# Sixteen tokens moved from the dense to the gathered path, and half of the experts' weight loads issued from ScalarE's queue

## The chip, the cores and the metric

The kernel runs on one core of a Trainium2 chip. The metric is device time in microseconds (us); the median of three runs of the kernel before is 2014.75 us (2012.73 to 2016.01). The engines are TensorE (PE, with its weight loads shown apart as PEld), VectorE (DVE), ScalarE (ACT), GpSimd (POOL) and SyncE (SP).

## The reference

One inference step of a one-layer transformer on 288 tokens (256 prompt tokens, 32 sampled ones) of width 2048 in float32: differential attention with a relative bias, cross-attention into 256 memory tokens, output projection, a first norm, and then a product-key expert layer:

```
q = (x1 @ w_q) -> 8 heads x 2 halves; s = q . sub_keys          # 128 keys in each half
16 best of each half -> 16 best of their 256 sums: expert = 128 * i1 + i2; gates = softmax(best)
act = x1 . u[expert]; h = gelu(act) * gate; y = sum h * v[expert]     # 128 experts of 16384 per token
out = layer_norm(ALPHA * x1 + y)
```

The tables u and v have 16384 rows of 2048 numbers each.

## The kernel before

Weights stream from DRAM in units of 128 x 1024 floats, 512 KB each, in the fixed order of the list `plan`. A unit goes through `raw` (four buffers, loaded by `load_next`), then ScalarE rounds it into `hi` (L165) and VectorE takes the rest into `lo` (L181), three buffers each; TensorE multiplies both, so that float32 is kept with the fast type. `take` gives TensorE the next unit; before that `stream` has emitted the `hi` of the unit two ahead and the loads of the units up to four ahead. A load waits until the `lo` of the unit four before it has been made, because they share a buffer. In the kernel before SP issues all these loads.

The expert layer treats the tokens in two ways.

- The dense tokens, ND = 224 of them, are multiplied with all experts. The key blocks i = 0 to 127 are two units each: 16 times a product of 448 columns (L1039, both parts of the tokens against `hi`) and one of 224 (L1041, against `lo`). `finish_act` adds the small products with a product by the identity (`small`, L992; L994) and applies gelu. From block 64 on (G0) `gate_jobs` spreads the gates over all experts, two tokens per unit: VectorE makes the one-hot rows of the second key, ScalarE makes those of the first by two activations a token (L974, L975), TensorE multiplies them, and `gate_in` puts the gates of four tokens into the activations (`bigA`, `bigB`): multiplied by VectorE where the activation is there, copied by VectorE where it is not. Then come 256 units of values, V: 8 pairs of products a unit (L1200, L1202) onto eight accumulators, in two halves of the columns.
- The other 64 tokens are gathered: for each of 64 slots, POOL fetches the two half rows of 128 experts (64 tokens by two groups of heads fill the 128 partitions) by an indirect DMA (L948), 512 KB a step and 128 steps for u and again for v, into three buffers; VectorE multiplies each with the token's row (`use_u`, L963) or adds it to `vacc` (`use_v`, L1111). The steps are spread evenly over the units by `upto`: GFIRST = 40 of u before block 64, the others until block 126, and those of v from about unit 9 to unit VEND = 230.

Beside the stream, `slow` holds work that VectorE does in small pieces, paced once per tick by an estimated cost: the top-16 search (`topk`), the choices, and at the end `finish_gathered`, which adds the halves of the gathered tokens, norms and stores them. It is begun when the last step of v has been emitted, and what is left of it is emitted at once in the last group of V (three units), ahead of the evacuation of the last eight accumulators (L1120). The norm rows of the dense tokens are loaded by it too, into `vacc`, and the last stage (`centred`, `finished`, `store`) needs them.

In `order`'s rows below, `hi_5<-raw_4` is the rounding of a unit, `DMA raw_4<-in_v` its load, `ohA` a first-key one-hot, `small` and `tmp` the steps of `finish_act`, `vr` a gathered half row, `x1g` the gathered tokens' rows (later `vacc`), `x1b` those of the added ones.

Of the kernel before, what the change touches and what calls it, by code (L numbers as in the profile page):

```python
# [21 lines left out]
ND = 224  # L22
# [13 lines left out]
SPLIT = 96  # L36
# [7 lines left out]
GFIRST = 40  # L44
# [5 lines left out]
def tile_stream_step(ctx: ExitStack, tc, xT_d, xn_d, memT_d, ckT_d, cv_d, cmkT_d, cmv_d,  # L50
# [54 lines left out]
    # ------------------------------------------------ the stream of everything large  # L105
# [36 lines left out]
    plan += [weight(wq_d[t, half]) for t in Q_TILES[2:] for half in range(2)]  # L142
    plan += [weight(ut_d[i, half]) for i in range(NKEY) for half in range(2)]
# [5 lines left out]
    def stream(n, ahead=AHEAD):  # L149
        """splits up to the weights that are ahead units after unit n, and loads beyond them"""  # L150
# [78 lines left out]
    def mm_tile(ps, part, k, d, mh, ml, n):  # L229
        """out^T [128 columns, n tokens] += one contraction tile of weights' (mh + ml)"""  # L230
# [5 lines left out]
    def mm_unit(ps, half, mh, ml, n, ticks=(3, 7), tiles=8):  # L236
        """the next unit's contraction tiles"""
# [54 lines left out]
    def bias_job():  # L292
        """the relative bias of all heads, laid out by diagonals through DRAM"""
# [35 lines left out]
    # ------------------------------------------------ mixers  # L329
# [45 lines left out]
    def diff_attend(h, qT, kT, vT, ck, cv):  # L375
# [51 lines left out]
        def weights(t):  # L427
            # w * s0 = e0 - lam * s0 / s1 * e1
# [155 lines left out]
    # ------------------------------------------------ output projection, first norm  # L584
# [27 lines left out]
    def residual(c, ps):  # L612
        """the tokens' rows again, added to the residual"""
# [3 lines left out]
                       ps[:, ND:NTOK].unsqueeze(1).to_broadcast([P, 2, 64]))  # L617
# [44 lines left out]
    # ------------------------------------------------ expert choice  # L662
    ROWS = (P, 96, P)

    def topk(units):
# [3 lines left out]
        st = []  # L669
        for q, (t, h, u) in enumerate(units):  # L670
            R = ROWS[t]

            def new(tag, shape, dt=F32, share=None, q=q, R=R, t=t, h=h):
                return tw.tile([P] + shape, dt, tag=f"{share or tag}{q}", name=f"{tag}{t}_{h}")[:R]
            st.append(dict(R=R, s=s_all[:R, u], sv=new("sv", [2, K]), si=new("si", [2, K], U32), sf=new("sf", [2, K]),
                           s2=new("s2", [2, NKEY]), ca=new("ca", [K, K]), new=new, pos=new("pos", [K], U32),
                           ab=new("ab", [2, K], U32), abf=new("abf", [2, K]), bv=best[:R, t, h],
                           en=(e1n[:R, t, h], e2n[:R, t, h])))
        n = len(units)
        both = [(x, c) for c in range(2) for x in st]  # L680
        for x, c in both:
            V.max(out=x["sv"][:, c, 0:8], in_=x["s"][:, c])
        for x, c in both:
            V.max_index(out=x["si"][:, c, 0:8], in_max=x["sv"][:, c, 0:8], in_values=x["s"][:, c])
            if c == 0 and x is st[-1]:
# [9 lines left out]
        for x, c in both:
            V.max_index(out=x["si"][:, c, 8:16], in_max=x["sv"][:, c, 8:16], in_values=x["s2"][:, c])
        for x in st:
            R = x["R"]
            V.tensor_tensor(out=x["ca"], in0=x["sv"][:, 0].unsqueeze(2).to_broadcast([R, K, K]),
                            in1=x["sv"][:, 1].unsqueeze(1).to_broadcast([R, K, K]), op=OP.add)  # L700
        yield 0.75 * n
        for x in st:
            V.tensor_copy(x["sf"], x["si"])
            x["cb"] = x["new"]("cb", [K, K], share="s2")
            x["cf"], x["c2"] = (x[k].rearrange("p a b -> p (a b)") for k in ("ca", "cb"))
        for x in st:
            V.max(out=x["bv"][:, 0:8], in_=x["cf"])
        yield 0.45 * n
        for x in st:
            V.match_replace(out=x["c2"], in_to_replace=x["bv"][:, 0:8], in_values=x["cf"], imm_value=-3.0e38)  # L710
        for x in st:
            V.max_index(out=x["pos"][:, 0:8], in_max=x["bv"][:, 0:8], in_values=x["cf"])
# [680 lines left out]
```

## Time and profile before

| | |
|---|---|
| median of three runs | 2014.75 us |
| span of the profiled execution, first to last instruction | 2008.1 us; that leaves 6.65 us to the median |
| busy: PE, PEld, DVE, ACT, POOL | 99%, 93%, 78%, 58%, 24% of the span |
| key blocks | first product 624.6 us; first gate product, in block 64, 960.4 us |
| values V | 1336 to 1990 us, the last stage to 2008.1 us |
| DMA, whole span | 521.21 MB, 260 GB/s |

A line of the page or of an answer names the line of the kernel, the engine, the operation and the tiles. "Idle before" is the time for which an engine waited ahead of an instruction, and the name behind the arrow is what ended that wait. A table by windows shows, for each stretch, the busy time of every engine with its count of instructions, the granted clock of TensorE as a share of full speed, the mean busy share of the 16 DMA engines and the rate at which they moved data.

### The profile page before, as it was taken

To read this page: it belongs to the slowest core of one execution; us is meant where nothing else is said; L and a number is where in the kernel's file an instruction comes from. 1 tells how busy PE (TensorE), PEld (TensorE's weight loads), DVE (VectorE), ACT (ScalarE), POOL (GpSimd) and SP (SyncE) were. 2 spreads that over 40 slices of the span, in tenths; PEclk is the share of its full clock that TensorE was granted. 3 is DMA by queue.
4 is the path that set the end of the run, shared out by engine and by line. 5 is a ranking of instruction groups with operands and counts; after the bars stand their busy time and mean duration, and the time that the engine had idled before them with its cause. 6 is when DMAs were issued, how large, how long until landed. Compare 5 with 4: busy or idle time off the path is not lost.

```text
span 2008.1 us, 34989 instructions
## 1 busy us (share of the span) xinstructions
PE 1983.6 (99%) x13178; PEld 1872.5 (93%) x13178; DVE 1567.3 (78%) x2683; ACT 1160.7 (58%) x1919; POOL 480.9 (24%) x348
## 2 busy tenths in 40 slices
PE   9999999999999999999999999999999999999996
PEld 7999999999999999999999999999999999999996
DVE  5455555556788889998899999978888888888886
ACT  5345545544534555555999999854455555444553
POOL 0110000010000112222333333324443343334412
PEclk9999999999999999999999999999999999999998
DMA  8854555484445788888888888889999998999985
GB/s 294 258 165 141 153 155 153 129 287 137 154 148 162 241 291 280 277 282 283 294 298 296 293 298 302 300 288 318 335 322 343 327 333 314 323 328 321 327 264 167
DMA packets 147625, 521.21 MB, mean 260 GB/s; under 512 B 16848, under 2 KB 21088, under 8 KB 147328
## 3 DMA queue, kind: packets, MB, share of 16 engines
q1 hardware_dynamic: 103504, 360.49, 54.8%
q0 software_dynamic: 43952, 158.48, 22.0%
q8 instruction: 104, 1.70, 0.3%
q14 instruction: 65, 0.53, 0.1%
HBM read 508.33 MB, written 10.06 MB: 258 GB/s over the span
## 4 chain that ended last, share of the span: by engine, by line
PE 96%; DMA 1%; DVE 1%; ACT 1%; POOL 0%; issue 0%; SPq 0%; POOLq 0%; ACTq 0%; DVEq 0%
PE pa L1039 22%; PE pa L1200 11%; PE pb L1200 11%; PE pa L1041 11%; PE pa L232 8%; PE pa L233 7%; PE pa L234 7%; PE pb L1202 5%; PE pa L1202 5%; PE pb L1019 3%; DMA raw<-in_wmk 1%; PE pa L994 1%; PE pb L397 0%; DVE lo L181 0%; PE pa L893 0%; PE pa L319 0%
## 5 line engine op out<-in xcount | busy, mean ns | idle before, releaser
L181 DVE TENSOR_TENSOR lo<-raw,hi 128x1024 fp32r<-128x1024 f32 (+1 forms) x679 | 820.8, 1211 | 367.1 <-ACT hi L165 356.7
L165 ACT CAST hi<-raw 128x1024 fp32r<-128x1024 f32 (+1 forms) x679 | 705.5, 1040 | 497.2 <-PE pa L1200 253.8
L1039 PE MATMUL pa<-ux,hi 128*128 128x448 f32 x2048 | 669.8, 379 | 0.0
L1041 PE MATMUL pa<-ux,lo 128*128 128x224 f32 x2048 | 543.6, 265 | 0.0
L1039 PEld LDWEIGHTS pa<-ux,hi 128*128 128x128 f32 x2048 | 385.4, 188 | 29.4 <-issue 0.2
L1041 PEld LDWEIGHTS pa<-ux,lo 128*128 128x128 f32 x2048 | 391.7, 191 | 0.0
L948 POOL DMA_INDIRECT ur<-in_u,gidx x128 | 197.9, 1546 | 700.2 <-DVE ur L963 329.8
L1200 PE MATMUL pa<-hs,hi 128*128 128x448 f32 x1020 | 338.3, 376 | 0.0
L1200 PE MATMUL pb<-hs,hi 128*128 128x448 f32 x1020 | 338.0, 376 | 0.0
L948 POOL DMA_INDIRECT vr<-in_v,gidx x128 | 221.4, 1730 | 354.7 <-DVE x1g L1111 321.2
L1202 PE MATMUL pb<-hs,lo 128*128 128x224 f32 x1020 | 271.1, 266 | 0.3 <-DVE lo L181 0.3
L1202 PE MATMUL pa<-hs,lo 128*128 128x224 f32 x1020 | 271.0, 266 | 0.0
L1200 PEld LDWEIGHTS pb<-hs,hi 128*128 128x128 f32 x1020 | 191.4, 188 | 17.5
L1200 PEld LDWEIGHTS pa<-hs,hi 128*128 128x128 f32 x1020 | 191.4, 188 | 17.4
L1202 PEld LDWEIGHTS pb<-hs,lo 128*128 128x128 f32 x1020 | 195.1, 191 | 0.5 <-DVE lo L181 0.5
L232 PE MATMUL pa<-xh,hi 128*128 128x288 f32 x640 | 195.2, 305 | 0.0
L1202 PEld LDWEIGHTS pa<-hs,lo 128*128 128x128 f32 x1020 | 195.1, 191 | 0.0
L233 PE MATMUL pa<-xl,hi 128*128 128x288 f32 x640 | 188.9, 295 | 0.0
L234 PE MATMUL pa<-xh,lo 128*128 128x288 f32 x640 | 188.2, 294 | 0.0
L1111 DVE SCALAR_TENSOR_TENSOR x1g<-vr,ggate,x1g 128x1024 f32<-128x1024 f32 x128 | 163.7, 1279 | 0.0
L963 DVE SCALAR_TENSOR_TENSOR ur<-ur,x1g 128x1024 f32<-128x1024 f32 x128 | 155.7, 1216 | 0.0
L232 PEld LDWEIGHTS pa<-xh,hi 128*128 128x128 f32 x640 | 120.0, 188 | 4.9 <-issue 3.7
(346 smaller groups left out, 2706.7 us busy)
## 6 DMA issues: line engine op xcount, KB each, us to landing
raw<-in_ut SPq DMA_DIRECT2D x256, 512.0 KB, 4.4
raw<-in_v SPq DMA_DIRECT2D x255, 512.0 KB, 6.5
raw<-in_win SPq DMA_DIRECT2D x80, 512.0 KB, 3.7
raw<-in_wq SPq DMA_DIRECT2D x32, 512.0 KB, 3.6
raw<-in_wo SPq DMA_DIRECT2D x29, 512.0 KB, 3.7
raw<-in_wmv SPq DMA_DIRECT2D x8, 512.0 KB, 5.3
raw<-in_wmk SPq DMA_DIRECT2D x6, 512.0 KB, 5.8
xn<-in_xn POOLq DMA_DIRECT2D x8, 384.0 KB, 9.7
```

The source lines that it names most:

```text
L165: nc.scalar.copy(hi[:, cs], raw[:, cs])
L181: nc.vector.tensor_sub(lo, raw, hi.bitcast(F32))
L232: nc.tensor.matmul(ps[:, :n], wh, mh[:, d, :n], start=(d == 0), stop=False)
L233: nc.tensor.matmul(ps[:, :n], wh, ml[:, d, :n], start=False, stop=False)
L234: nc.tensor.matmul(ps[:, :n], wl, mh[:, d, :n], start=False, stop=(d == DT - 1))
L948: nc.gpsimd.indirect_dma_start(out=t, out_offset=None, in_=self.table, in_offset=bass.IndirectOffsetOnAxis(ap=gidx[:, a, s:s + 1], axis=0))
L963: nc.vector.scalar_tensor_tensor(rows, rows, 1.0, x1g[:, a * 1024:(a + 1) * 1024], op0=OP.mult, op1=OP.mult, accum_out=gact[:, a, s:s + 1])
L1039: nc.tensor.matmul(ps[:, :2 * ND], wh, ux[:, d].rearrange("p a t -> p (a t)"), start=(d == 0), stop=False, skip_group_check=True)
L1041: nc.tensor.matmul(ps[:, :ND], wl, ux[:, d, 0], start=False, stop=False, skip_group_check=True)
L1111: nc.vector.scalar_tensor_tensor(va, rows, ggate[:, s:s + 1], va, op0=OP.mult, op1=OP.add)
L1200: nc.tensor.matmul(accs[dt][:, :2 * ND], wh, hb.rearrange("p a t -> p (a t)"), start=(i == 0), stop=False, skip_group_check=True)
L1202: nc.tensor.matmul(accs[dt][:, :ND], wl, hb[:, 0], start=False, stop=False, skip_group_check=True)
```

## The change

ND becomes 208 and 80 tokens are gathered: the 64 of before, and the 16 tokens 208 to 223, each of which has its eight heads in eight groups of partitions and 16 further slots (`x1b`). There are 160 steps for u and for v instead of 128. The dense products have 416 and 208 columns instead of 448 and 224, and there are 104 gate jobs for two tokens instead of 112. The pieces of `topk` work on two heads in one instruction where they can; the second key's one-hots are made for four tokens at once; the copies of `gate_in` go from VectorE to ScalarE. `finish_gathered` has four foldings instead of one and a move of 16 rows. Every odd unit from the first key block on is loaded from ScalarE's queue.

```diff
-ND = 224
+ND = 208
+NA = 224
+SLOTS = 80
+STEPS = 2 * SLOTS
-SPLIT = 96
+SPLIT = 88
-GFIRST = 40
+GFIRST = 48
...
+    UFIRST = len(plan)
     plan += [weight(ut_d[i, half]) for i in range(NKEY) for half in range(2)]
...
+            queue = nc.scalar if k >= UFIRST and k % 2 else nc.sync
             for cs in pieces(k):
-                nc.sync.dma_start(raw[:, cs], src[:, cs])
+                queue.dma_start(raw[:, cs], src[:, cs])
...
     def gate_in(t0, ps, done):
...
             if a < n:
-                nc.vector.tensor_copy(bt[:, a:n, t0:t0 + 4], pg[:, i0 + a:i0 + n])
+                nc.scalar.copy(bt[:, a:n, t0:t0 + 4], pg[:, i0 + a:i0 + n])
...
+    def second_hots(t0):
+        Bt = big[2].tile([P, 4, NKEY], F32, tag="ohB", name=f"ohB{t0}")
+        nc.vector.tensor_tensor(out=Bt, in0=iota.unsqueeze(1).to_broadcast([P, 4, NKEY]),
+                                in1=e2T[:, t0:t0 + 4].unsqueeze(2).to_broadcast([P, 4, NKEY]), op=OP.is_equal)
+        return Bt
...
-                    ug.upto(GFIRST + (128 - GFIRST) * (n + 1 - 2 * G0) // (2 * (NKEY - G0) - 4))
+                    ug.upto(GFIRST + (STEPS - GFIRST) * (n + 1 - 2 * G0) // (2 * (NKEY - G0) - 4))
...
     def use_v(s, a, rows):
-        va = vacc[:, a * 1024:(a + 1) * 1024]
+        va = (vacc if s < 64 else x1b)[:, a * 1024:(a + 1) * 1024]
         nc.vector.scalar_tensor_tensor(va, rows, ggate[:, s:s + 1], va, op0=OP.mult, op1=OP.add)
...
     def finish_gathered():
-        up = [gat.tile([P, 1024], F32, tag="rows", name=f"up{c}") for c in range(2)]
-        for c in range(2):
-            nc.gpsimd.dma_start(up[c][:64], vacc[64:128, c * 1024:(c + 1) * 1024])
+        for x, w in ((vacc, 64), (x1b, 64), (x1b, 32), (x1b, 16)):
+            up = [gat.tile([P, 1024], F32, tag="rows", name=f"up{num()}") for c in range(2)]
+            for c in range(2):
+                nc.gpsimd.dma_start(up[c][:w], x[w:2 * w, c * 1024:(c + 1) * 1024])
+            yield 4.0
+            for c in range(2):
+                cs = slice(c * 1024, (c + 1) * 1024)
+                nc.vector.tensor_add(x[0:w, cs], x[0:w, cs], up[c][:w])
+                yield 1.15
+        nc.gpsimd.dma_start(vacc[64:SLOTS], x1b[0:16])
         yield 4.0
-        v = vacc[0:64]
...
+        v = vacc[0:SLOTS]
...
-                vg.upto(128 * (n + 1 - v_from) // (VEND - v_from))
+                vg.upto(STEPS * (n + 1 - v_from) // (VEND - v_from))
```

On ScalarE in the values, the kernel before has this order (one `hs` in four units):

```order
L165 CAST hi_16790<-raw_16743 128x1024
L165 CAST hi_16815<-raw_16768 128x1024
L165 CAST hi_16840<-raw_16793 128x1024
L165 CAST hi_16862<-raw_16818 128x1024
L75 CAST hs_16884<-bigA 128x4x224
```

and the changed kernel this one:

```order
L169 CAST hi_21056<-raw_21015 128x1024
L196 DMA raw_21059<-in_v 128x1024
L78 CAST hs_21079<-bigB 128x4x208
L169 CAST hi_21082<-raw_21037 128x1024
L169 CAST hi_21105<-raw_21059 128x1024
L196 DMA raw_21108<-in_v 128x1024
L169 CAST hi_21131<-raw_21085 128x1024
L169 CAST hi_21153<-raw_21108 128x1024
```

The load of each odd unit now stands behind the rounding of the odd unit ahead of it: raw_21108 is issued behind the instruction that reads raw_21059.

On ScalarE in the key blocks from 64 on, one block (two units) before:

```order
L992 CAST small_12880<-pa_12802 128x224
L165 CAST hi_12883<-raw_12806 128x1024
L1000 ACTIVATE tmp_12906<-pa_12802 128x112
L1002 ACTIVATE bigA<-pa_12802 128x112
L974 ACTIVATE ohA_12910<-iota,e1T 128x128
L975 ACTIVATE ohA_12910<-ohA_12910,gT,ngT 128x128
L974 ACTIVATE ohA_12910<-iota,e1T 128x128
L975 ACTIVATE ohA_12910<-ohA_12910,gT,ngT 128x128
L165 CAST hi_12918<-raw_12844 128x1024
```

and the second half of such a block in the changed kernel:

```order
L169 CAST hi_13076<-raw_13001 128x1024
L196 DMA raw_13079<-in_ut 128x1024
L981 ACTIVATE ohA_13099<-iota,e1T 128x128
L982 ACTIVATE ohA_13099<-ohA_13099,gT,ngT 128x128
L981 ACTIVATE ohA_13099<-iota,e1T 128x128
L982 ACTIVATE ohA_13099<-ohA_13099,gT,ngT 128x128
L994 COPY bigB<-pb_13026 128x31x4
L999 CAST small_13113<-pa_13037 128x208
```

A load and a copy of the gates (two of them below block 88) are new among ScalarE's instructions there; the copy waits for VectorE's multiplication out of the same bank.

On VectorE at the end of the values, the kernel before goes from the last `lo` to the accumulators:

```order
L181 TENSOR_TENSOR lo_21651<-raw_21604,hi_21650 128x1024
L181 TENSOR_TENSOR lo_21682<-raw_21629,hi_21681 128x1024
L181 TENSOR_TENSOR lo_21702<-raw_21653,hi_21701 128x256 x4
L1120 SCALAR_TENSOR_TENSOR yT<-yT,pb_18636 128x224
L1120 SCALAR_TENSOR_TENSOR yT<-yT,pb_18639 128x224
```

and the changed kernel, in two pieces with the norm's six smallest steps between them:

```order
L185 TENSOR_TENSOR lo_21512<-raw_21466,hi_21511 128x1024
L185 TENSOR_TENSOR lo_21532<-raw_21488,hi_21531 128x256 x4
L1161 TENSOR_TENSOR x1b<-x1b,up_21412 16x1024
L1169 BN_STATS nst_21545<-x1g 80x6 x4
L1143 BN_AGGR nmr_21546<-nst_21545 80x2
```

```order
L1145 SCALAR_TENSOR_TENSOR nmr_21546<-nmr_21546 80x1
L1179 TENSOR_TENSOR x1g<-x1g,gb_21543 80x1024
L1181 TENSOR_TENSOR x1g<-x1g,gb_21544 80x1024
L1179 TENSOR_TENSOR x1g<-x1g,gb_21568 80x1024
L1181 TENSOR_TENSOR x1g<-x1g,gb_21569 80x1024
L1135 SCALAR_TENSOR_TENSOR yT<-yT,pb_18445 128x208
```

The last folding and the whole norm of the gathered tokens stand ahead of the first accumulator's evacuation.

## Rows read from the trace of the kernel before

**Rows 1.** Busy time by stretch: the columns are us, engines, clock, DMA share, GB/s.

```profile
640.00:950.00 310.00, 310.00 (x1986) 294.64 (x1985) 275.88 (x650) 170.62 (x253) 58.37 (x41) 1.00 0.82 273
960.00:1290.00 330.00, 330.00 (x2235) 315.67 (x2234) 302.65 (x587) 310.25 (x708) 121.42 (x77) 1.00 0.85 297
1360.00:1640.00 280.00, 280.00 (x1770) 264.83 (x1770) 235.82 (x202) 139.66 (x139) 114.43 (x71) 1.00 0.94 331
1680.00:1900.00 220.00, 220.00 (x1391) 207.96 (x1390) 185.39 (x158) 110.14 (x109) 88.80 (x50) 1.00 0.93 326
```

**Rows 2.** Timeline of PE in three stretches: start, duration, instruction.

```profile
43.73 0.40 PE L320 MATMUL pa<-hi,meml 128*128 128x512 f32 x1
59.13 0.40 PE L320 MATMUL pa<-hi,meml 128*128 128x512 f32 x1
...
641.44 0.37 PE L1039 MATMUL pa<-ux,hi 128*128 128x448 f32 x1
645.82 0.37 PE L1039 MATMUL pa<-ux,hi 128*128 128x448 f32 x1
```

**Rows 3.** Timeline of ACT, key block 87 to 88.

```profile
1100.43 0.33 ACT L992 CAST small<-pa 128x224 fp32r<-128x224 f32 x1
...
1101.94 0.25 ACT L1000 ACTIVATE tmp<-pa 128x92 f32<-128x92 f32 x1 [0.23 <-PE pa L994]
...
1106.49 0.32 ACT L992 CAST small<-pa 128x224 fp32r<-128x224 f32 x1
```

**Rows 4.** Groups by line and shape, 1360 to 1640 us: count, busy, mean ns, idle before.

```profile
L181 DVE TENSOR_TENSOR lo<-raw,hi 128x1024 fp32r<-128x1024 f32 x111 | 135.9, 1225 | 44.2 <-ACT hi L165 40.8
L165 ACT CAST hi<-raw 128x1024 fp32r<-128x1024 f32 x111 | 116.8, 1052 | 140.8 <-PE pa L1200 109.7 <-DMA raw<-in_v 23.5 <-DVE lo L181 4.0
...
L1111 DVE SCALAR_TENSOR_TENSOR x1g<-vr,ggate,x1g 128x1024 f32<-128x1024 f32 x63 | 80.6, 1280 | 0.0
L76 DVE TENSOR_TENSOR hs<-bigA,hs 128x896 fp32r<-128x896 f32 x21 | 22.8, 1086 | 0.0
```

**Rows 5.** Busy time by stretch, two stretches of 20 us.

```profile
640.00:660.00 20.00, 20.00 (x130) 19.04 (x129) 19.30 (x59) 10.81 (x16) 0.00 (x0) 1.00 0.69 202
1420.00:1440.00 20.00, 20.00 (x129) 18.93 (x128) 16.19 (x14) 10.10 (x10) 8.42 (x6) 1.00 0.97 350
```

**Rows 6.** DMA issues, 1360 to 1640 us: count, KB each, median us to landing.

```profile
raw<-in_v SPq DMA_DIRECT2D x110, 512.0 KB, 6.7
```

**Rows 7.** DMA issues, 520 to 620 us.

```profile
raw<-in_wq SPq DMA_DIRECT2D x23, 512.0 KB, 3.6
```

**Rows 8.** Line 191, SP's queue, 1500 to 1520 us: duration ns min/median/max of one issue.

```profile
L191 SPq DMA_DIRECT2D raw<-in_v x8: 327/328/328, 1501.0 to 1519.6; - x8
```

**Rows 9.** Timeline of DVE at the end.

```profile
1939.46 0.26 DVE L1128 BATCH_NORM_AGGREGATE nmr<-nst 64x2 f32<-64x24 f32 x1
...
1942.21 0.15 DVE L1130 SCALAR_TENSOR_TENSOR nmr<-nmr 64x1 f32<-64x1 f32 x1
...
1979.56 1.43 DVE L181 TENSOR_TENSOR lo<-raw,hi 128x256 fp32r<-128x256 f32 x4 [0.66 <-ACT hi L165]
1981.87 0.39 DVE L1120 SCALAR_TENSOR_TENSOR yT<-yT,pb 128x224 f32<-128x224 f32 x1 [0.88 <-PE pb L1119]
...
1993.11 0.74 DVE L1287 SCALAR_TENSOR_TENSOR fo<-pb,mr,x1g 128x512 f32<-128x512 f32 x1
```

**Rows 10.** The tile x1g from 1925 us on: duration ns min/median/max, landing of its DMAs.

```profile
L1151 DVE BATCH_NORM_STATS2 nst<-x1g x4: 665/676/681, 1934.0 to 1938.7; 64x6 f32<-64x512 f32 x4
...
L1146 DVE TENSOR_TENSOR x1g<-x1g,up x2: 1208/1208/1209, 1928.1 to 1931.7; 64x1024 f32<-64x1024 f32 x2
...
L1159 ACT ACTIVATE x1g<-x1g,nmr x2: 1241/1242/1242, 1942.9 to 1963.3; 64x1024 f32<-64x1024 f32 x2
L1161 DVE TENSOR_TENSOR x1g<-x1g,gb x2: 1208/1208/1209, 1946.7 to 1966.6; 64x1024 f32<-64x1024 f32 x2
...
DMA to landing us min/median/max: 3.2/5.9/7.1
```

**Rows 11.** The tile gb: landing of its DMAs.

```profile
DMA to landing us min/median/max: 7.3/7.9/9.4
```

More of the change, by code (lines that the diff above doesn't have):

```diff
@@ L582, in tile_stream_step @@
     xs.close()
+    x1b = ctx.enter_context(tc.tile_pool(name="late", bufs=1)).tile([P, D], F32, tag="x1b", name="x1b")
     x1s = ExitStack()
@@ L663, in tile_stream_step @@
     ROWS = (P, 96, P)
+    DENSE = (P, ND - P)
     def topk(units):
         V = nc.vector
[L669 to L685, printed above, removed]
+        n, t, R = len(units), units[0][0], ROWS[units[0][0]]
+        key = f"{t}_{units[0][1]}"
+        step = units[-1][1] - units[0][1] or 1
+        hs = slice(units[0][1], units[-1][1] + 1, step)
@@ new lines, in new @@
+        def new(tag, shape, dt=F32):
+            return tw.tile([P, 2] + shape, dt, tag=tag, name=f"{tag}{key}")[:R, :n]
+        S = [s_all[:R, u] for *_, u in units]
+        sv, si, sf = new("sv", [2, K]), new("si", [2, K], U32), new("sf", [2, K])
+        s2, ca, pos = new("s2", [2, NKEY]), new("ca", [K, K]), new("pos", [K], U32)
+        ab, abf = new("ab", [2, K], U32), new("abf", [2, K])
+        bv = best[:R, t, hs]
+        both = [(q, c) for c in range(2) for q in range(n)]
+        for q, c in both:
+            V.max(out=sv[:, q, c, 0:8], in_=S[q][:, c])
@@ L686, in topk @@
+        for q, c in both:
+            V.max_index(out=si[:, q, c, 0:8], in_max=sv[:, q, c, 0:8], in_values=S[q][:, c])
+            if c == 0 and q == n - 1:
                 yield 0.64 * n
         yield 0.22 * n
-        for x, c in both:
-            V.match_replace(out=x["s2"][:, c], in_to_replace=x["sv"][:, c, 0:8], in_values=x["s"][:, c],
-                            imm_value=-3.0e38)
+        for q, c in both:
+            V.match_replace(out=s2[:, q, c], in_to_replace=sv[:, q, c, 0:8], in_values=S[q][:, c], imm_value=-3.0e38)
@@ L691, in topk @@
         yield 0.43 * n
-        for x, c in both:
-            V.max(out=x["sv"][:, c, 8:16], in_=x["s2"][:, c])
+        for q, c in both:
+            V.max(out=sv[:, q, c, 8:16], in_=s2[:, q, c])
         yield 0.43 * n
[L695 to L712, printed above, removed]
@@ L736, in topk @@
-        yield 0.7 * n
-        for c, key in ((0, "ca"), (1, "cb")):
-            for x in st:
-                V.tensor_reduce(out=x["en"][c], in_=x[key], op=OP.add, axis=AX.X)
-        yield 0.7 * n
+        for q, c in both:
+            V.max_index(out=si[:, q, c, 8:16], in_max=sv[:, q, c, 8:16], in_values=s2[:, q, c])
+        V.tensor_tensor(out=ca, in0=sv[:, :, 0].unsqueeze(3).to_broadcast([R, n, K, K]),
+                        in1=sv[:, :, 1].unsqueeze(2).to_broadcast([R, n, K, K]), op=OP.add)
@@ new lines, in topk @@
+        yield 0.7 * n
+        V.tensor_copy(sf.rearrange("p q c k -> p (q c k)"), si.rearrange("p q c k -> p (q c k)"))
+        cf = [ca[:, q].rearrange("p a b -> p (a b)") for q in range(n)]
+        c2 = [s2[:, q].rearrange("p a b -> p (a b)") for q in range(n)]
+        for q in range(n):
+            V.max(out=bv[:, q, 0:8], in_=cf[q])
+        yield 0.4 * n
+        for q in range(n):
+            V.match_replace(out=c2[q], in_to_replace=bv[:, q, 0:8], in_values=cf[q], imm_value=-3.0e38)
@@ new lines, in topk @@
+        for q in range(n):
+            V.max_index(out=pos[:, q, 0:8], in_max=bv[:, q, 0:8], in_values=cf[q])
+        yield 0.7 * n
+        for q in range(n):
+            V.max(out=bv[:, q, 8:16], in_=c2[q])
+        yield 0.35 * n
+        for q in range(n):
+            V.max_index(out=pos[:, q, 8:16], in_max=bv[:, q, 8:16], in_values=c2[q])
+        V.tensor_scalar(ab[:, :, 0], pos, 4, None, op0=OP.logical_shift_right)
+        V.tensor_scalar(ab[:, :, 1], pos, 15, None, op0=OP.bitwise_and)
@@ L742, in gates @@
+        yield 0.62 * n
+        for c, en in ((0, e1n), (1, e2n)):
+            V.tensor_reduce(out=en[:R, t, hs], in_=eq[c], op=OP.add, axis=AX.X)
+        yield 0.62 * n
     def gates(t, nh):
@@ L1006, in gate_jobs @@
     def gate_jobs():
-        hots, banks = {}, {}
+        first, second, banks = {}, {}, {}
         n2 = ND // 2
@@ L1093, in tile_stream_step @@
     vacc = x1g
+    only16 = vw.tile([P, 1], F32, tag="only16", name="only16", bufs=1)
     def gathered_h():
```

135 lines of the change are left out of this document (65 added, 70 removed).

## The prediction

> **What bounds the kernel now.** I read the table of busy times by stretch first, over the 1360 us of the expert layer, since only there the change touches what repeats. In all four stretches TensorE is busy without a gap at full granted clock (1.00, the 2.4 GHz level) [rows 1]: it sets the pace, and fewer columns should shorten the layer. The same rows show how little is left beside it. In key blocks 0 to 63 VectorE is busy 275.9 of 310 us (0.89). From block 64 on VectorE has 302.7 and ScalarE 310.3 of 330 us (0.92 and 0.94). In the values the DMA engines are at 0.94 and 0.93. So each stage has a second engine within 6 to 11% of TensorE, and the change takes 7% off TensorE and adds work to each of the three. What counts is which one is late next. For that I read the timeline of ScalarE in a block, the groups of the values with their waits, and the landing times.
>
> **What TensorE could give back.** 66 products of 512 columns start within 59.13 - 43.73 = 15.40 us, 233.3 ns each; 14 pairs of 448 and 224 columns within 645.82 - 641.44 = 4.38 us, 312.9 ns a pair [rows 2]. A straight line through both is 9.8 ns + 0.437 ns a column, so a pair of 416 and 208 takes 292 ns, 21 ns less. There are 2048 pairs in the key blocks and 2048 in the values: 43 us in each, 86 us in all. A product of 208 columns with a new weight does not occur in the trace; if its weight load did not fit, the small product would stay as it is and the gain be two thirds. This is the ceiling; what follows takes it stage by stage.
>
> **Key blocks 0 to 63.** 64 x 16 x 21 ns = 21.5 us are to be had. VectorE's work at the shorter pace: 0.89 / 0.933 = 0.95 of the time, and it gets 8 more steps of u (48 for 40), by the values' 1.28 us [rows 4] some 10 us, and a top-16 unit for the new tokens, against which the joined instructions save about as much. That is 0.97 to 0.98 of an engine that also waits for ScalarE's `hi`. I take half of the gain: -11 us (bounds -21.5 and 0).
>
> **Key blocks 64 to 127.** ScalarE's block here lasts from one `small` to the next, 1106.49 - 1100.43 = 6.06 us, and it waits only 0.23 us in it, for TensorE [rows 3]: 5.83 us of its own. TensorE, which sets the 6.06 us, would need 16 x 21 ns = 0.34 us less, 5.72 us. The change adds to ScalarE's block one or two copies of gates out of PSUM (like `small`, 0.33 us a piece [rows 3], mostly smaller), and their wait for VectorE's multiplication: the copy stands behind four one-hot activations, about as long as the `lo` and the multiplication take on VectorE, so I put 0.1 to 0.2 us for it. 5.83 + 0.2 + 0.15 = 6.2 us: ScalarE becomes the bound, and the 52 blocks with gates gain nothing and lose 0.14 us each, +7 us. Behind the waiting copy stand `small`, on which TensorE's next identity product waits, and the next `hi`. The issue itself, 327 ns on SP [rows 8], follows a rounding of 1.05 us [rows 4] whose run covers it; uncovered it would be 0.33 us x 64 = 21 us. Four blocks fewer have one-hots, each worth about 0.95 us: -4 us. The last 12 blocks, free of gates, should run at TensorE's 4.75 us, but fetch 2 units and 112 / 62 = 1.8 steps, 3.8 x 0.524 MB = 2.0 MB; the fastest stretch of 20 us shows 350 GB/s at a share of 0.97 [rows 5], which makes 5.7 us, where such a block takes 5.1 us before (16 x 312.9 ns and the identity product): +7 us. In all +10 us (bounds -19, if all of TensorE's gain came, and +29 with the issue uncovered).
>
> **Values.** A unit lasts 280 / 111 = 2.52 us now [rows 4]; TensorE alone would need 8 x 21 = 0.17 us less, 2.36. Some 221 units also carry gathered steps: 160 / 221 = 0.72 a unit, where 0.58 were. A unit then moves 1.72 x 0.524 = 0.904 MB. At 2.36 us that is 383 GB/s; these stretches run at 331 and 326 GB/s with a share of 0.94 and 0.93 [rows 1], and the highest 20 us at 350 [rows 5]. At 350 GB/s the unit takes 2.58 us, 0.06 more than now. VectorE has 1.225 + 0.72 x 1.28 + 1.086 x 0.93 / 4 = 2.40 us a unit [rows 4], so even without the DMA limit only 0.12 us can be gained.
>
> The second limit is the new queue. On ScalarE the load of an odd unit is issued behind the rounding of the odd unit before it, and that rounding waits for its own load. So there is never more than one odd load in flight, and two units cannot take less than one landing. Before, SP keeps 6.7 / 2.52 = 2.7 loads in flight and each lands after 6.7 us [rows 6]; alone, in the query projection, one lands after 3.6 us [rows 7]. Between 3.6 and 6.7 I take the middle, 5.2 us for two units, since the wait behind loads of its own queue goes and the sharing with SP's loads and the gathers stays. That is 2.6 us a unit and agrees with the bytes. By 2.58 us, 221 x 0.06 = +13 us; 35 units without steps gain 0.16 us each, -5.5 us. Together +8 us (bounds: VectorE's pace, 221 x -0.12 - 5.5 = -32 us; the old landing with the issue on top, (6.7 + 0.33) / 2 = 3.5 us a unit, +211 us).
>
> Is the issuing queue a bound now? One issue takes 327 ns [rows 8] of a unit of 2.52 us, 13%: no. The Trainium skill (DMA: Bandwidth & Descriptors, Rules for kernel authors) speaks against the edit in the same sense: transfers from SP, ACT and GpSimd run on the same 16 engines, so that spreading them saves only issue time. By that rule the second queue is worth nothing, and the trace's 13% agrees. The same page (Specifications) gives about 358 GB/s of HBM for one core; by that estimate a unit would take 2.53 us and the values gain 3 us, where the row of 350 GB/s gives 2.58.
>
> **The end.** `finish_gathered` starts at unit 229 as before, but its estimated cost grows from about 22 to about 45 ticks, one per unit, and only 24 are left. So the last folding, the move of 16 rows and the norm are emitted in the last group, on VectorE ahead of the evacuations. After the last `lo` they form one chain: an addition 1.2, the move 3.2 (the fastest landing of that tile), four statistics 2.7, ScalarE's scaling 1.2, product and sum 2.4, product and sum of the second half 2.4 [rows 10]; the small steps of the norm, from 1939.46 to 1942.36, 2.9 [rows 9]; the second half's gain row, issued after the first half's sum, 7.3 [rows 11] and some 1.6 us of issues by POOL ahead of it. Sum 24.9 us. Before, the first evacuation starts 0.9 us after the last `lo` (1979.56 + 1.43 to 1981.87) and the last stage 11.2 us later, at 1993.11 [rows 9]. In the meantime TensorE can finish its first accumulators, which saves some 3 or 4 us of those 11. So +20 us (bounds +10, were the gain rows to land as fast as 3.2 us [rows 10] and more overlapped, and +26).
>
> What lies ahead of the key blocks (an eight-fold copy of 16 rows, four more passes of 1.2 us on VectorE beside TensorE's products) I put at nothing; uncovered it is 5 us.
>
> **Sum.** -11 + 10 + 8 + 20 = +27 us on the profiled span of 2008.1 us: 2035 us, and with the 6.65 us by which the median of 2014.75 us exceeds that span, 2042 us.
>
> **Rivals.**
> - Three queues let the DMA engines carry more than the 350 GB/s seen. For it: at 202 GB/s of weights alone the share is 0.69 (293 GB/s at full share), at 350 it is 0.97 (361) [rows 5], so a mix of queues uses the engines better, and a third may go on. Then VectorE sets 2.41 us in the values: -30 us instead of +8, the last key blocks lose their 7, the first ones gain 3 more. -14 + 3 - 30 + 20 = -21: 1994 us, faster.
> - The chain of odd loads decides: landing stays near 6 us because three queues share the engines. It decides from a landing of 5.05 us, two units as they are now. With 6.0 us and the issue, 3.17 us a unit: 221 x 0.65 = +144 us for the +13, 2173 us; with 5.5 it is 2.92 us, +88 us and 2117 us. Against it: the last key blocks and the projection, where fewer loads queue, land earlier [rows 7].
> - The gain comes as meant, because VectorE, ScalarE and the DMA engines all hold TensorE's new pace: -86 + 20 = -66, 1949 us. Against it stand three rows of 0.92 to 0.94 [rows 1].
> - The terms cancel within 4 us: about 2015 us.
>
> **Chances.** My forecast with its neighbours, 2022 to 2070 us, 0.54; more engines' rate, 0.20; all of the gain, 0.04; the chain of loads, 0.14; cancelled, 0.08. The range of 8 in 10 is 1992 to 2100 us; the forecast's own is 2022 to 2070. What differs by less than 0.2% (4 us) a measurement of this kernel can hardly tell from no change. Faster 0.25, same 0.08, slower 0.67.
>
> **What would show it.** Right: in key blocks from 64 on ScalarE has no wait for TensorE but one for VectorE ahead of the copy, and a block of 6.1 to 6.3 us; in the values TensorE waits, ScalarE's rounding waits for `raw`, and the rate is near 350 GB/s; odd loads land in about 5 us; from the last `lo` to the first evacuation VectorE runs some 25 us of the norm, with TensorE idle. Wrong: values at 380 GB/s with no waits on TensorE, or odd loads at 4 us or less; a tail no longer than before; blocks from 64 on under 5.9 us.

## The result: 11% slower, and where the profile after shows it

Median 2242.75 us (2234.33 to 2245.79) against 2013.95 us for the kernel before on the same chip: 1.1135 times as long, 95% interval 1.1110 to 1.1161. The direction was as predicted; the time lies far above 2042 us and above the range.

I cut both executions at five events: the first product of the key blocks, the first product of the gates, the first product of the values, the start of the last `lo`, the end of the span. The first four stand in the views of single lines (count, ns min/median/max, first and last start in us). The kernel before:

```profile
L1039 PE MATMUL pa<-ux,hi x2048: 368/374/475, 624.6 to 1335.7; 128*128 128x448 f32 x187
...
L1019 PE MATMUL pb<-ohA,ohB x448: 274/275/281, 960.5 to 1297.3; 128*128 128x128 f32 x150
...
L1200 PE MATMUL pb<-h,hi x4: 370/374/376, 1336.0 to 1337.1; 128*128 128x448 f32 x4
...
L181 DVE TENSOR_TENSOR lo<-raw,hi x679: 415/1225/1290, 6.1 to 1980.6; 128x1024 fp32r<-128x1024 f32 x166, 128x256 fp32r<-128x256 f32 x2, 128x512 fp32r<-128x512 f32 x1, 128x768 fp32r<-128x768 f32 x1
```

The same lines of the kernel after:

```profile
L1050 PE MATMUL pa<-ux,hi x2048: 362/368/589, 625.8 to 1388.6; 128*128 128x416 f32 x187
...
L1029 PE MATMUL pb<-ohA,ohB x416: 275/275/348, 977.5 to 1315.8; 128*128 128x128 f32 x139
...
L1219 PE MATMUL pb<-h,hi x4: 366/477/588, 1388.9 to 1394.2; 128*128 128x416 f32 x4
...
L185 DVE TENSOR_TENSOR lo<-raw,hi x679: 414/1224/1280, 6.5 to 2189.0; 128x1024 fp32r<-128x1024 f32 x166, 128x256 fp32r<-128x256 f32 x2, 128x512 fp32r<-128x512 f32 x1, 128x768 fp32r<-128x768 f32 x1
```

The differences of these starts are the stages. The table has them for the kernels of the experiments too, which are explained below (us of the profiled execution):

| kernel | ahead | key blocks 0–63 | 64–127 | values | end | span |
|---|---|---|---|---|---|---|
| before | 624.6 | 335.9 | 375.5 | 644.6 | 27.5 | 2008.1 |
| after | 625.8 | 351.7 | 411.4 | 800.1 | 49.5 | 2238.5 |
| e1 80 tokens, SP | 625.4 | 324.9 | 384.9 | 646.3 | 50.4 | 2031.9 |
| e2 64 tokens, ACT | 628.3 | 349.8 | 379.3 | 775.4 | 26.9 | 2159.7 |
| e3 loads ahead | 632.2 | 328.6 | 410.9 | 649.1 | 49.1 | 2069.9 |
| e4 early end | 628.8 | 327.0 | 386.2 | 654.6 | 28.2 | 2024.8 |
| e5 copies on DVE | 629.2 | 325.4 | 365.7 | 642.6 | 50.8 | 2013.7 |
| e6 e3 and e5 | 627.1 | 326.9 | 387.5 | 651.9 | 50.1 | 2043.5 |
| e7 72 tokens | 645.0 | 330.3 | 396.8 | 645.7 | 28.7 | 2046.5 |
| e8 72, copies on DVE | 644.0 | 330.4 | 368.6 | 639.2 | 27.1 | 2009.3 |
| e9 e5, early end | 627.7 | 327.6 | 364.2 | 651.9 | 28.7 | 2000.1 |
| e10 72, fewer DMAs | 637.2 | 331.3 | 369.4 | 637.3 | 28.5 | 2003.7 |

Of the 230 us, 156 are in the values, 16 and 36 in the two halves of the key blocks, 22 at the end. Busy time by stretch of the kernel after, with the columns of [rows 1]:

```profile
640.00:950.00 310.00, 292.70 (x1907) 284.95 (x1906) 274.68 (x612) 156.00 (x242) 71.25 (x46) 0.99 0.80 271
980.00:1310.00 330.00, 306.90 (x2067) 292.72 (x2068) 289.15 (x461) 299.83 (x731) 115.83 (x92) 1.00 0.88 307
1440.00:1780.00 340.00, 292.74 (x1729) 273.60 (x1729) 243.58 (x212) 130.08 (x135) 127.19 (x84) 0.94 0.83 289
1850.00:2100.00 250.00, 208.57 (x1226) 190.51 (x1225) 173.05 (x150) 90.92 (x95) 74.56 (x55) 0.96 0.81 279
```

In the values every engine has become slack at once: TensorE 292.7 of 340 us at a granted clock of 0.94 (a mean of stretches at 2.4 and at 1.2 GHz), where it had no gap at 1.00, VectorE 0.72, ScalarE 0.38, and the DMA engines 0.83 at 289 GB/s where they had 0.94 and 331. Nothing is full, so something waits in a circle. The page's chain that ended last gives the line:

```profile
DMA raw<-in_v 29%; DMA raw<-in_ut 14%; PE pa L237 7%; PE pa L238 7%; PE pa L239 7%; PE pa L1050 6%; DVE lo L185 3%; PE pa L1052 3%; ACT hi L169 2%; PE pa L1219 2%; PE pb L1219 1%; DVE ur L966 1%; PE pb L1221 1%; PE pa L1221 1%; DVE bigA L99
```

Waits from 1440 to 1780 us (engine, line waited for, us in total, times, longest), and the DMA issues of the same stretch (count, KB, median us to landing):

```profile
ACT hi L169 <- DMA raw<-in_v: 184.7, 51, 7.1
DVE lo L185 <- ACT hi L169: 89.2, 41, 5.5
...
PE pb L1221 <- DVE lo L185: 26.9, 39, 0.8
...
PE pb L1219 <- ACT hi L169: 19.9, 18, 2.9
```

```profile
raw<-in_v ACTq DMA_DIRECT2D x54, 512.0 KB, 6.2
raw<-in_v SPq DMA_DIRECT2D x54, 512.0 KB, 6.1
```

TensorE waits for the parts, the parts for ScalarE's rounding, the rounding for `raw`. The timeline of ScalarE and its queue shows why the loads are late though the engines have room:

```profile
1507.58 1.06 ACT L169 CAST hi<-raw 128x1024 fp32r<-128x1024 f32 x1 [2.02 <-DMA raw<-in_v]
1507.61 0.33 ACTq L196 DMA_DIRECT2D raw<-in_v  x1
...
1515.71 1.06 ACT L169 CAST hi<-raw 128x1024 fp32r<-128x1024 f32 x1 [3.41 <-DMA raw<-in_v]
1515.73 0.34 ACTq L196 DMA_DIRECT2D raw<-in_v  x1
```

The odd load issued at 1507.61 stands behind the odd rounding of 1507.58; it has landed at 1515.71, the next odd rounding starts that moment, and only then does the next odd load go out. Two units take 8.1 us here. On average they take 2 x 340 / 108 = 6.30 us, and the median landing of an odd load is 6.2 us: the period is the landing. In all of this stretch no odd load goes out before the one ahead of it has landed, and the median pause between landing and issue is 0.12 us; 45 of the 54 odd roundings had to wait for `raw`, and 6 of the 53 even ones.

### The profile page after: what moved, and what is told of

Same layout as the page of the kernel before. It is cut to its first block, busy times and chain, and to the rows that moved or that the text cites. A ratio compares the mean times of both kernels' runs of the same rounds, so it can differ in the third digit from the quotient of the medians.

```text
span 2238.5 us, 34941 instructions
## 1 busy us (share of the span) xinstructions
PE 2024.2 (90%) x13146; PEld 1909.2 (85%) x13146; DVE 1621.8 (72%) x2569; ACT 1137.9 (51%) x1962; POOL 534.8 (24%) x437
## 4 chain that ended last, share of the span: by engine, by line
DMA 44%; PE 40%; DVE 7%; ACT 5%; issue 3%; POOL 0%; ACTq 0%; SPq 0%; DVEq 0%; POOLq 0%
DMA raw<-in_v 29%; DMA raw<-in_ut 14%; PE pa L237 7%; PE pa L238 7%; PE pa L239 7%; PE pa L1050 6%; DVE lo L185 3%; PE pa L1052 3%; ACT hi L169 2%; PE pa L1219 2%; PE pb L1219 1%; DVE ur L966 1%; PE pb L1221 1%; PE pa L1221 1%; DVE bigA L992 1%
## 5 line engine op out<-in xcount | busy, mean ns | idle before, releaser
L1050 PE MATMUL pa<-ux,hi 128*128 128x416 f32 x2048 | 644.1, 373 | 0.0
L1052 PE MATMUL pa<-ux,lo 128*128 128x208 f32 x2048 | 532.0, 260 | 2.0 <-DVE lo L185 1.9
L1219 PE MATMUL pb<-hs,hi 128*128 128x416 f32 x1020 | 353.3, 387 | 44.5 <-ACT hi L169 44.0
L950 POOL DMA_INDIRECT vr<-in_v,gidx x160 | 241.6, 1510 | 494.2 <-DVE x1g L1126 389.0
L950 POOL DMA_INDIRECT ur<-in_u,gidx x160 | 219.2, 1370 | 527.8 <-DVE ur L966 318.9
L1219 PE MATMUL pa<-hs,hi 128*128 128x416 f32 x1020 | 341.9, 382 | 0.0
L1221 PE MATMUL pb<-hs,lo 128*128 128x208 f32 x1020 | 283.6, 278 | 63.6 <-DVE lo L185 63.3
L1221 PE MATMUL pa<-hs,lo 128*128 128x208 f32 x1020 | 272.0, 267 | 0.0
L1219 PEld LDWEIGHTS pb<-hs,hi 128*128 128x128 f32 x1020 | 202.3, 198 | 59.8 <-ACT hi L169 56.7
L1219 PEld LDWEIGHTS pa<-hs,hi 128*128 128x128 f32 x1020 | 201.8, 198 | 2.4
```

The lines of the kernel that those rows point to most:

```text
L950: nc.gpsimd.indirect_dma_start(out=t, out_offset=None, in_=self.table, in_offset=bass.IndirectOffsetOnAxis(ap=gidx[:, a, s:s + 1], axis=0))
L1050: nc.tensor.matmul(ps[:, :2 * ND], wh, ux[:, d].rearrange("p a t -> p (a t)"), start=(d == 0), stop=False, skip_group_check=True)
L1052: nc.tensor.matmul(ps[:, :ND], wl, ux[:, d, 0], start=False, stop=False, skip_group_check=True)
L1219: nc.tensor.matmul(accs[dt][:, :2 * ND], wh, hb.rearrange("p a t -> p (a t)"), start=(i == 0), stop=False, skip_group_check=True)
L1221: nc.tensor.matmul(accs[dt][:, :ND], wl, hb[:, 0], start=False, stop=False, skip_group_check=True)
```

## The experiments

**e1: the queue undone.** The kernel after with

```
-            queue = nc.scalar if k >= UFIRST and k % 2 else nc.sync
+            queue = nc.sync
```

> 80 gathered tokens, all expert loads on SP's queue again. Theory (one odd load at a time on ScalarE's queue is what costs): the values fall from 3.24 us a unit to about 2.55, nearly all of the 229 us goes, and the time is that of my sum without the queue, 2042 us (2010 to 2060); the rounding no longer waits for raw in the values. Rival (the 16 further tokens cost it: more bytes, ScalarE's copies of gates, the longer tail): above 2150 us, and the key blocks from 64 on keep their 6.45 us a block.

Measured: 2034.74 us, 1.0119 times before (1.0092 to 1.0145). The theory held, but for one sign that is taken up below. Row by row the table shows what the queue cost: 27 us in key blocks 0–63, 26 in 64–127, 154 in the values, nothing at the end. What remains are the four terms of my sum. Of the rival one part is right: the blocks from 64 on fell to no less than 6.2 to 6.44 us. First the stretches, with the columns of [rows 1]:

```profile
640.00:950.00 310.00, 308.79 (x2055) 305.38 (x2054) 290.40 (x635) 176.16 (x268) 86.81 (x51) 1.00 0.86 296
955.00:1270.00 315.00, 304.58 (x2053) 290.46 (x2052) 284.95 (x458) 294.76 (x724) 129.46 (x91) 1.00 0.91 319
1440.00:1640.00 200.00, 193.66 (x1264) 188.74 (x1264) 179.08 (x157) 98.32 (x100) 102.47 (x62) 1.00 0.98 361
1640.00:1900.00 260.00, 250.02 (x1615) 242.43 (x1614) 228.08 (x205) 126.47 (x133) 128.38 (x72) 0.99 0.95 346
```

Then one such block on ScalarE, the answer to [rows 3]:

```profile
1120.18 0.34 ACT L999 CAST small<-pa 128x208 fp32r<-128x208 f32 x1
...
1126.33 0.28 ACT L994 COPY bigB<-pb 128x144 f32<-128x144 f32 x1 [0.33 <-DVE bigB L992]
1126.51 0.34 ACT L999 CAST small<-pa 128x208 fp32r<-128x208 f32 x1
```

6.33 us from one `small` to the next, no wait for TensorE any more, but one of 0.33 us for VectorE's multiplication ahead of the copy. TensorE is full in the first key blocks (308.8 of 310 us) and the DMA engines in the values (0.98 and 0.95). The sign that failed: the rounding still waits for `raw` there, 83.4 us in the 200 from 1440 on, where it waited 20.0 us in the kernel before. So a wait for `raw` does not tell a circle from full DMA engines; their share does, 0.98 here and 0.83 in the kernel after.

**e2: the queue alone.** The kernel before with the line `queue = nc.scalar if k >= UFIRST and k % 2 else nc.sync`.

> The kernel before (64 gathered tokens, 224 dense) with every second expert load on ScalarE's queue and nothing else changed. Theory (chain of odd loads): the queue alone does the damage. The gathers are fewer (0.58 steps a unit), so a landing is somewhat shorter than 6.2 us, and a unit takes 2.9 to 3.1 us instead of 2.52: the values 85 to 130 us longer, the key blocks 20 to 40, in all 2120 to 2190 us. Rival (the 80 tokens): under 2030 us.

Measured: 2162.87 us, 1.0769 times before (1.0712 to 1.0827). The queue alone costs 150 us, 131 of them in the values; the key blocks lose 18, a little under the 20 to 40 expected. Odd loads land after a median of 5.8 us from 1440 to 1900 us, and two units take 6.05 us (152 in 460 us). Key blocks 64–127 lose 3.8 us against the 26 with 80 tokens: here landings are shorter (5.1 us from 980 to 1300 us, in a block of 6.06) and ScalarE had 0.23 us of slack in a block [rows 3].

**e3: the same queues, another order.** In `stream`, from the experts on, the loads are issued ahead of the rounding:

```
+        if n >= UFIRST:
+            while at["load"] <= min(until + RAW - AHEAD, len(plan) - 1):
+                load_next()
         while at["split"] <= until:
```

> The changed kernel, except that each load is issued ahead of the rounding that stands at the same place, not behind it: the same two queues, the same bytes and the same number of issues, but two odd loads may be in flight. Theory (it is the place behind the waiting rounding, not the queue): 2015 to 2060 us, the values near 2.55 us a unit, with landings of odd loads of 6 to 9 us that nobody waits for. Rival (loads on ScalarE's queue are slow in themselves, since it shares the DMA engines with SP's and the gathers, or their issue takes ScalarE's time): above 2150 us with rounding still waiting for raw.

Measured: 2071.00 us, 1.0291 times before (1.0257 to 1.0326), so between the theory's 2060 and the rival's 2150. In the values the theory is shown: 649.1 us where the kernel after takes 800.1, with the same loads on ScalarE's queue:

```profile
raw<-in_v ACTq DMA_DIRECT2D x90, 512.0 KB, 6.7
```

```profile
1440.00:1640.00 200.00, 192.83 (x1243) 185.70 (x1243) 175.91 (x153) 95.88 (x97) 102.46 (x62) 1.00 0.97 355
```

A landing of 6.7 us, longer than the 6.2 of the kernel after, now costs next to nothing, because the load goes out one rounding earlier and has nearly three units instead of two. ScalarE still waits for `raw`, 92.5 us in these 200, about as much as in e1, and TensorE hardly notices. Of the 38 us by which the span exceeds e1's, 26 are in key blocks 64–127 and 7 ahead of the key blocks, where the two kernels are the same. From 980 to 1300 us:

```profile
ACT hi L172 <- DMA raw<-in_ut: 18.9, 21, 2.5
...
raw<-in_ut ACTq DMA_DIRECT2D x48, 512.0 KB, 7.2
```

```profile
1124.31 0.34 ACTq L199 DMA_DIRECT2D raw<-in_ut  x1
1124.74 1.05 ACT L172 CAST hi<-raw 128x1024 fp32r<-128x1024 f32 x1
...
1131.56 1.05 ACT L172 CAST hi<-raw 128x1024 fp32r<-128x1024 f32 x1 [0.45 <-DMA raw<-in_ut]
```

ScalarE is the bound there, its block lasts 6.2 to 6.44 us when nothing is late, and the median odd load lands after 7.2 us. The load of 1124.31 goes out only 0.43 us ahead of the odd rounding, because four one-hot activations stand in front of both: in these blocks the edit moved the issue by half a microsecond, not by a whole rounding. Its own rounding is due 6.8 us later, waits 0.45 us for it and starts at 1131.56. Such waits are 18.9 us in these 320; that they are paid in full because ScalarE has no slack is a theory, which e6 tries.

**e4: the norm ahead of the last group.** e1 with

```
                     slow.append(finish_gathered())
+                    pace["rate"] = 2.2
```

> 80 tokens, all loads on SP, and the small jobs beside the values go 2.2 times as fast once the last gathered row is used, so that the last foldings and the norm of the gathered rows are done ahead of the last group instead of in front of the evacuations. Theory (that norm is a chain of some 20 us at the end): 15 to 24 us less than with SP's loads alone, with the first evacuation about 1 us behind the last small part. Rival (the tail is long for another reason, or the jobs only delay the small parts instead): within 6 us of it.

Measured: 2027.17 us, 1.0066 times before (1.0047 to 1.0084); 7.6 us less than e1, not 15 to 24. The end itself did what the theory said, 50.4 to 28.2 us. But the values took 8.3 us more. In one stretch of 10 us TensorE stood for half of it, because on VectorE the first folding waits 3.37 us for its moved rows, with a `lo` behind it; later the second gain row holds up a `lo` by 5.11 us in the same way:

```profile
1930.00:1940.00 10.00, 4.51 (x19) 4.28 (x19) 6.57 (x6) 2.44 (x3) 1.03 (x2) 0.66 0.95 220
```

```profile
1933.21 1.22 DVE L1161 TENSOR_TENSOR x1g<-x1g,up 64x1024 f32<-64x1024 f32 x1 [3.37 <-DMA up<-x1g]
1934.35 1.21 DVE L185 TENSOR_TENSOR lo<-raw,hi 128x1024 fp32r<-128x1024 f32 x1
...
1981.83 1.22 DVE L1179 TENSOR_TENSOR x1g<-x1g,gb 80x1024 f32<-80x1024 f32 x1 [5.11 <-DMA gb<-in_lnrow]
1982.97 1.22 DVE L185 TENSOR_TENSOR lo<-raw,hi 128x1024 fp32r<-128x1024 f32 x1
```

Another 6.8 us lie ahead of the values, where the two kernels are the same, 3.4 of them ahead of the key blocks: the spread of these stages from one execution to the next (624.6 to 632.2 us ahead of the key blocks with 64 and 80 tokens).

**e5: the copies of gates back on VectorE.** e1 with

```
-                nc.scalar.copy(bt[:, a:n, t0:t0 + 4], pg[:, i0 + a:i0 + n])
+                nc.vector.tensor_copy(bt[:, a:n, t0:t0 + 4], pg[:, i0 + a:i0 + n])
```

> 80 tokens, all loads on SP, and the copies of gates out of PSUM on VectorE again instead of ScalarE. Theory (with the copies ScalarE is the bound of key blocks 64 to 127: its block there grows from 6.2 to 6.44 us and it waits for nothing but VectorE's multiplication): without the copies of 0.29 and 0.20 us and their wait a block falls to 5.8 to 6.05 us, 10 to 20 us less than with SP's loads alone. Rival (VectorE, which is busy 0.90 there and gets 73 copies of 0.25 us, or the DMA engines at 0.91 are as late): the same time within 6 us, blocks of 6.2 us or more, and VectorE without a gap.

Measured: 2015.45 us, 1.001 times before (0.9988 to 1.0031), 19 us less than e1, all of it in key blocks 64–127. TensorE has the stage again, and VectorE, at 0.99, just holds it:

```profile
955.00:1270.00 315.00, 314.60 (x2199) 312.20 (x2199) 312.09 (x561) 298.87 (x680) 169.46 (x97) 1.00 0.95 341
```

**e6: loads ahead, copies on VectorE.** The edits of e3 and e5 together; the odd loads are on ScalarE's queue.

> Odd loads on ScalarE's queue, issued ahead of the rounding, and the copies of gates on VectorE. With the loads ahead alone the key blocks 64 to 127 still took 411 us, with blocks that waited for raw standing between blocks as long as with SP's loads. Theory (ScalarE has no slack there, so each late landing is paid in full): with 0.45 us of slack in each block the late landings are absorbed in part, the stage takes 385 to 400 us, the kernel 2045 to 2060 us. Rival (loads on ScalarE's queue land late whatever ScalarE does): the stage stays above 405 us.

Measured: 2045.90 us, 1.0153 times before (1.0129 to 1.0177); the stage 387.5 us. The numbers held, the reason is not shown. The stage fell by 23 us against e3, but 19 of these come without the queue too (e5 against e1): of the 26 us that the queue costs in the stage with the copies on ScalarE, 22 remain without them. From 980 to 1250 us ScalarE's waits for `raw` did fall, from 14.9 us in e3 to 5.9, but VectorE, which e5 shows at 0.99, now waits 14.7 us for gathered rows, where e5 has no such wait. So the rival is not excluded: with the second queue something still comes late, if less often `raw`, and why stays open. So do the 9 us that the values take over e5.

**e7 and e8: 72 tokens.** `ND = 216`, `SLOTS = 72`; the 8 further tokens have 16 copies of their rows, and half of their choices in each half of the partitions; one-hots of two tokens instead of four and single buffers, to fit; rate 1.5, `VEND = 220`. e8 also has e5's edit.

> 72 gathered tokens (216 dense), all loads on SP, the gathered rows used up by unit 220 and the last jobs 1.5 times as fast. Theory (each second engine is passed a little later than TensorE's gain comes: with 80 tokens the values are at 0.98 and 0.95 of the DMA engines, with 64 at 0.93): the values gain 10 to 20 us on both neighbours (TensorE's unit of 2.44 us, bytes of 1.65 times 0.524 MB at 350 GB/s 2.47 us), the first key blocks 5, the end stays at 28 us: 1985 to 2005 us, faster than before. Rival (16 short steps of folding and the steps of 1.28 us on VectorE, 144 for 128, eat it): 2010 to 2030 us.

> The same with 72 tokens, and the copies of gates on VectorE. Theory: 4 to 12 us less than with the copies on ScalarE, 1975 to 1998 us, since 72 tokens leave VectorE more room than 80. Rival (VectorE is as late): the same within 4 us.

Measured: e7 2039.66 us, 1.0114 times (1.0075 to 1.0153); e8 2010.17 us, 0.9986 (0.9973 to 0.9999). I expected 1985 to 2005 and 1975 to 1998: both missed. The values gained 5 us at most where I expected 10 to 20, and the key blocks began 19 us later. In e7 the blocks from 64 on were worse than with 80 tokens (396.8 us); e8 lost 28 us of that with the copies, where I expected 4 to 12. Since the one-hots and the buffers changed along with the number of tokens, these two runs do not tell which of them spoiled the blocks.

**e9: the two gains together.** 80 tokens, SP, e5's edit, rate 1.5 and `VEND = 222`.

> 80 tokens, all loads on SP, copies of gates on VectorE, the gathered rows used up by unit 222 and the last jobs 1.5 times as fast: the two gains found so far together. Theory (they lie in different stages and add): 2015 us less the 22 us of the chain at the end, plus up to 8 us for foldings that TensorE waits for: 1993 to 2004 us, 0.5 to 1% faster than before. Rival (with the end free, the denser gathers, 0.74 steps a unit at 0.98 of the DMA engines, cost what the end gives): 2008 us or more.

Measured: 1999.46 us, 0.9931 times before (0.9918 to 0.9945), 0.7% faster than before and as expected. The end gave its 22 us, the values took 9 back.

**e10: 72 tokens with fewer copies.** e8 with 8 copies of rows and of scores and one copy of half the tile, for 16 each.

> The kernel of 72 tokens with copies of gates on VectorE, and the 16 copies of 8 rows (x1b) and the 16 of scores replaced by 8 and one copy of half the tile. With 16, the key blocks began 15 to 19 us later than with 64 or 80 tokens. Theory (the small copies of rows delay the loads of the projection): the key blocks begin at 625 to 632 us again, the time is 1990 to 1998 us. Rival (the late start comes from elsewhere): 2005 us or more.

Measured: 2002.45 us, 0.995 times before (0.9937 to 0.9963), between the theory's range and the rival's. The key blocks begin at 637.2 us: 7 us came back, some 9 did not, and their cause stays open.

## Why the prediction was wrong, step by step

**The step that failed** is in the values: "Between 3.6 and 6.7 I take the middle, 5.2 us for two units". It measured 6.2 us, and two units 6.30. I had the circle (one odd load in flight, two units not under one landing) and the price per unit, and moved its landing halfway towards that of a stretch without gathers [rows 7], although in the values the gathers share the engines; the row of the stretch itself said 6.7 [rows 6]. That loads on their own queue would land earlier than behind others of one queue had no row to support it. The rival's 3.17 us a unit was near the measured 3.15, in part by luck: its landing of 6.0 was 0.2 us short and its issue added 0.33 that did not come. That the forecast of 2.6 "agrees with the bytes" was no support: bytes bound the unit from below, the circle bounds it too, and the later one decides.

**A second step was missing.** I priced the circle in the values alone. In the key blocks it costs 27 and 26 us more (e1): in the first half two units take some 5 us, the median odd load lands after 4.8 and just fits, and the late ones are paid; in the second the median landing is 6.1 us (980 to 1310 us) beside a block of ScalarE of some 6.3 that has no slack. But half of the 26 us, 12.8, lies behind the last gate product, where ScalarE has slack and waits: from there to the first product of the values the kernel after takes 73.1 us (1315.8 to 1388.9) and e1 60.3 (1274.9 to 1335.2). The line of e1, and the waits of the kernel after from 1316 to 1388 us:

```profile
L1029 PE MATMUL pb<-ohA,ohB x416: 275/275/291, 950.3 to 1274.9; 128*128 128x128 f32 x139
```

```profile
ACT hi L169 <- DMA raw<-in_ut: 33.0, 8, 5.7
```

With these 53 us the rival's 2173 us would have been 2226, near the 2243 measured.

**The issue** was rightly put at little: the row of 1507.61 starts 0.03 us behind the start of the rounding, so it runs beside it; adding 0.33 us to the landing, as the rival did, was too much.

**TensorE's gain was mis-sized by a third.** I took 21 ns a pair from a straight line through products of 512 columns and pairs. Ten pairs of e1:

```profile
701.69 0.37 PE L1050 MATMUL pa<-ux,hi 128*128 128x416 f32 x1
...
704.71 0.37 PE L1050 MATMUL pa<-ux,hi 128*128 128x416 f32 x1
```

3.02 us for ten, 302 ns a pair. That is also the median of key blocks 0–63, where the kernel before has 315 (the 312.9 of [rows 2] come from a stretch of 4 us); in the values the medians are 316 and 300. So the gain is 13 and 16 ns a pair, not 21. The weight loads, on PEld, show where the rest went; the kernel before and then e1:

```profile
700.58 0.19 PEld L1039 LDWEIGHTS pa<-ux,hi 128*128 128x128 f32 x1
700.69 0.19 PEld L1041 LDWEIGHTS pa<-ux,lo 128*128 128x128 f32 x1
700.90 0.19 PEld L1039 LDWEIGHTS pa<-ux,hi 128*128 128x128 f32 x1
```

```profile
702.80 0.19 PEld L1050 LDWEIGHTS pa<-ux,hi 128*128 128x128 f32 x1
702.91 0.19 PEld L1052 LDWEIGHTS pa<-ux,lo 128*128 128x128 f32 x1
703.10 0.19 PEld L1050 LDWEIGHTS pa<-ux,hi 128*128 128x128 f32 x1
```

The small product runs between the first start and the second, and that interval stays: a median of 108 ns with 224 columns, 108 with the 216 of e8 and 109 with 208. The interval of the large product shrinks, from 207 to 193 ns. That is the case I had named, the weight load that does not fit, with a gain of two thirds. The Trainium skill (TensorE: Matmul & The Clock Gate, Part 2) puts the load of P columns of weights at P / 1.2 ns, which for 128 columns makes an estimate of 107 ns, and the trace's 108 and 109 agree. The ceiling was some 60 us, not 86.

**The other terms, from e1.** Key blocks 0–63: -11.0 us, forecast -11, and that they meet is luck: I halved a gain of 21.5 us for VectorE's sake, but only 64 x 16 x 13 ns = 13 us were to be had, and TensorE, busy 308.8 of 310 us, got 11 of them. Blocks 64–127: +9.4, forecast +10, with errors that cancel. The 52 blocks with gates cost 11 us more (314.6 to 326.0), not 7, since ScalarE's block is 6.2 to 6.44 us, not 6.2; e5 shows that the copies are the cause, and 5.84 us, not 5.72, is TensorE's. The last 12 blocks gain 2 us where I had -4 and +7: they take 5.36 us each, not 5.7. (The term's upper bound of +29 should be 10 + 21 = +31; nothing rests on it.) Values: +1.7, forecast +8; the 220 units from the tenth on take 559.0 us before and 560.7 in e1, so a unit grew from 2.54 to 2.55 us, not from 2.52 to 2.58. Bytes were the limit as I had it, but it lay higher: 361 GB/s in the 200 us from 1440 on, where I took 350. The end: +22.9, forecast +20, with a chain of 21.4 us for the 24.9 summed; e4 shows that this chain is what the end consists of:

```profile
1981.81 1.21 DVE L1161 TENSOR_TENSOR x1b<-x1b,up 16x1024 f32<-16x1024 f32 x1
...
2000.82 1.22 DVE L1179 TENSOR_TENSOR x1g<-x1g,gb 80x1024 f32<-80x1024 f32 x1 [6.53 <-DMA gb<-in_lnrow]
...
2003.22 0.92 DVE L1135 SCALAR_TENSOR_TENSOR yT<-yT,pb 128x208 f32<-128x208 f32 x3
```

21.4 us from the folding to the first evacuation, 6.5 of them for the gain row. What lies ahead of the key blocks I put at nothing: +0.8. So without the queue the sum of 2042 us would have come near the 2034.74 of e1, in part because these errors cancel.

**The rival of more carrying queues** fell: e3 has three queues in the values and e1 two, at 355 and 361 GB/s in the same stretch of 200 us and 649.1 and 646.3 us. The Trainium skill's rule on this (DMA: Bandwidth & Descriptors, Rules for kernel authors: more issuing engines save only issue time) agrees with these rows; the harm in the values is another matter: it comes from the place at which the load is issued, since e3, with the same loads on the same queue, takes 2.8 us more than e1 there and not 154.

## What to carry to other kernels

A load that is issued by a computing engine leaves only when the instruction ahead of it lets it (here 0.03 us behind that one's start); if that instruction waits for the load before it, the loop cannot run faster than one landing for each turn, however idle the DMA engines are (here 0.83 busy). Before such a move, write down for each load what it is issued behind and how many units it is ahead of its use, and compare that lead with the landing in the same stretch, with all its other transfers, not in a quieter one. And when a loop slows while every engine, the DMA engines too, shows slack, look for that circle: one timeline of the waiting engine with its own queue shows it.

## What was not expected of the hardware

A product of 208 columns with a new weight buys nothing over one of 224: the two weight loads around it start 0.11 us apart with either. With SP's loads and the gathers alone the DMA engines carried 361 GB/s over 200 us at a share of 0.98; the highest 20 us before were 350 [rows 5]. And where TensorE waits, its clock falls too: in the values of the kernel after the granted clock is 0.94 and 0.96 in the mean, and the mean product of 416 columns takes 387 and 382 ns over all of the values, where e1, at 1.00 and 0.99, shows 369 and 368:

```profile
L1219 PE MATMUL pb<-hs,hi 128*128 128x416 f32 x1020 | 353.3, 387 | 44.5 <-ACT hi L169 44.0
L1219 PE MATMUL pa<-hs,hi 128*128 128x416 f32 x1020 | 341.9, 382 | 0.0
```
